# S5 inputs from x times g, the merge in two streams, and the recurrence's preparation cut into lanes of its own

## The chip, the cores and the metric

The kernel runs on one core of one Trainium2 chip. The metric is the device time of one execution in microseconds (us). TensorE (PE) does the matrix products; VectorE (DVE), ScalarE (ACT) and GpSimd (POOL) do the rest, and SyncE (SP) issues most of the transfers.

## The reference

One layer of a decoder, for 1024 tokens of width 1024 in float32:

```python
h = rms_norm(x, norm_mix_pre)              # x * rsqrt(mean(x*x) + 1e-6) * g, per token
proj = h @ w_in                            # columns: RWKV (1792), S5 input (512), gates (2048)
gates = sigmoid(proj[gate columns] + b_gate)
o_rwkv = rwkv7_branch(RWKV columns, ...) @ w_branch_rwkv
o_s5 = s5_branch(S5 columns, ...) @ w_branch_s5
mixed = (g_rwkv * o_rwkv + g_s5 * o_s5) @ w_out
x = x + rms_norm(mixed, norm_mix_post)
x = x + rms_norm(conv_ffn(rms_norm(x, norm_ffn_pre)), norm_ffn_post)
```

The RWKV-7 branch is a recurrence over the tokens with a 64x64 state for each of 8 heads. Each step scales the state by a decay, adds a product along a normalised key, and adds an outer product of value and key; then the state is multiplied by r. The S5 branch is a diagonal complex state space model (64 states for each group of 16 channels), followed by a GELU and a sigmoid GLU. The norm's factor 1/rms is one number per token, so h = (x * g) / rms, and a column of h @ w_in equals (x * g) @ w_in divided by rms afterwards.

## The kernel before

*Layout.* Activations lie channel-major: 128 channels on the partitions by 512 tokens, in two token halves (th = 0, 1). A product of float32 precision is made of three products of reduced width: each operand is split into a high part (a cast) and a low part (the difference), and PE adds hi*Whi, lo*Whi and hi*Wlo (`mm3_steps`, L171 to L173; the words "products" below are single ones of 128x128 by 128x512). Weights come through `load_w` (L143): a transfer, a cast on ACT (L155) and a subtraction on DVE (L156). Activations are split by `split` (L225, L226).

*Order.* PE executes in exactly the order in which the program emits its instructions. `drive` (L184) makes that order: it holds *lanes*, generators that each yield a PE cost and a latency (the constants T_... at the file's end, in us) or a condition. A lane whose latency has passed in the planner's own clock is continued; between lanes, the planner takes units of a background list, `fill`, one after the other, paced by PACE and CREDIT. If nothing is ready and fill is empty, the clock jumps. On the other engines a scheduler orders the instructions by dependence and priority (HP, HP2, HPW, HPN); each engine then executes its queue in order.

*Stages.*
1. Start (`load_x`, `norm`). x is loaded by SP, squared on ACT (L898), summed in pairs on DVE (L899) and over channels by PE (into the tile chk). From this the small steps of 1/rms are made, spread to a tile rbc, and DVE makes h = x * g * rbc (L908), which is split: high parts on ACT, low parts on DVE or, for every second tile, GpSimd.
2. S5 inputs (`s5_in`, L999): four column blocks of w_in times both halves of h, 192 products. ACT copies each result out with a change of layout (L1007); it is stored to DRAM, and SP reloads it as `u8` (`load_u8`) in S5's layout.
3. S5 itself (`s5_lane`, `tab_lane`): tables for each block (with transposes on PE at L543), then the state products. `mix_in` is the fill here: the projections of the RWKV columns, their low-rank second factors, and writing them to DRAM.
4. Recurrence. Four units i = 0..3, each for four heads (group i % 2) and one half (i // 2). For each there are: two *fronts* (`rwkv_front`, one per pair of heads u), which load r, k and v, normalise k and make the Gram products (L700) that DVE masks (L702); an *inverse* (`rwkv_inv`), which sends 32x32 blocks by transfers into another layout, runs 31 pairs of dependent DVE instructions (L757, L759), and sends the result back; the *natural layouts* (`rwkv_nat`), which are transposes on PE; the *level* step (`rwkv_level`), which begins with a DVE transpose of the inverse (L781) and joins 32-blocks to 64-blocks (L783 on PE); the *chain* (`rwkv_chain`) of eight dependent steps over 64 tokens each; and the *output* (`rwkv_out`) with a norm on DVE (L855) and transposes on PE (L861). `prep_lane` emits the fronts of unit i and, after the second, its inverse, and starts unit i+1's fronts only once the natural layouts of unit i are emitted. `chain_lane` emits natural layouts, level, chain and output in turn. The fill is the gate products (`gate_tiles`), and after the output of unit 1, `merge` and `outproj` for the first half.
5. `merge` (L1054) for the first half: eight tiles of the RWKV branch's projection times its gate, with the S5 GLU tiles put between, and then eight tiles of the S5 branch's projection times its gate, added to the first ones and split.
6. The second half's merge, the output projection, the norms and the gated FFN with its convolution. These stay as they are.

The two buffer pools `hp[0]` and `hp[1]` hold the split operands of each half, and the merge, the output projection and the fast FFN products use their slots again.

Of the kernel before, what the change touches and what calls it, by code (L numbers as in the profile page):

```python
# [9 lines left out]
F32 = mybir.dt.float32  # L10
# [60 lines left out]
class Kern:  # L71
# [71 lines left out]
    def load_w(self, *srcs):  # L143

        nc = self.nc
        wh, wl = [], []
        with self.tc.high_priority(HPW):
            for src in srcs:
                for o in range(0, src.shape[1], 512):
                    n = min(512, src.shape[1] - o)  # L150
                    h = self.wp.tile([128, 512], F32R, tag="wh", name=self.nm("wh"), bufs=NWH)
                    l = self.wp.tile([128, 512], F32R, tag="wl", name=self.nm("wl"), bufs=NWL)
                    f = self.wp.tile([128, 512], F32, tag="wf", name=self.nm("wf"), bufs=NWF)
                    nc.sync.dma_start(f[:, :n], src[:, o:o + n])
                    nc.scalar.copy(h[:, :n], f[:, :n])  # L155
                    nc.vector.tensor_tensor(l[:, :n], f[:, :n], h[:, :n].bitcast(F32), ALU.subtract)  # L156
                    wh.append(h)
                    wl.append(l)
        return wh, wl
# [114 lines left out]
    def setup(self):  # L274
        nc = self.nc
        self.vecs = self.const.tile([128, NVEC], F32, name="vecs")
        self.csts = self.const.tile([128, NCST], F32, name="csts")
        nc.gpsimd.dma_start(self.csts[:, 0:128], self.a["cst"][:, 0:128])
        nc.gpsimd.dma_start(self.vecs, self.a["vec"])
# [602 lines left out]
    def load_x(self, th, pool):  # L882
        xs = []
        for k in range(NK):
            x = pool.tile([128, 512], F32, name=self.nm("x"), tag="x", bufs=16)
            self.nc.sync.dma_start(x, self.a["x"][k * 128:k * 128 + 128, th * 512:th * 512 + 512])
            xs.append(x)
        return xs

    def norm(self, th, xs, pool):  # L890

        nc = self.nc
        ss = self.chk()[:, 0:512]
        yield 0, T_X
        for k in range(0, NK, 2):
            sq = [pool.tile([128, 512], F32, tag="sq", name=self.nm("sq"), bufs=4) for _ in range(2)]
            for i in range(2):
                nc.scalar.activation(sq[i], xs[k + i], AF.Square)  # L898
            nc.vector.tensor_tensor(sq[0], sq[0], sq[1], ALU.add)  # L899
            self.sumsq(ss, sq[0], k == 0)  # L900
            yield 0.9, 1.0
        bc = self.chk()[:, 0:512]
        self.spread(bc, self.rstd(ss, 1e-6, 1.0 / D))
        rbc = pool.tile([128, 512], F32, tag="rbc", name=self.nm("rbc"), bufs=1)
        nc.scalar.copy(rbc, bc)
        h = []
        for k in range(NK):
            nc.vector.scalar_tensor_tensor(xs[k], xs[k], self.vec("g_mix_pre", k), rbc, ALU.mult, ALU.mult)  # L908
            h.append(self.hsplit(xs[k], k, self.hp[th], eng=nc.gpsimd if k % 2 else nc.vector))
        self.h[th] = h  # L910
        yield 1.7, 5.0
# [45 lines left out]
    def rkv(self, p):  # L957

        for mt in (4 + p, p, 8 + p):
# [3 lines left out]
            yield from self.inproj((mt, use))  # L963

    def mix_in(self):
# [10 lines left out]
        self.load_u8(self.stored)  # L976
# [16 lines left out]

    def load_u8(self, b):

        self.nc.sync.dma_start(self.u8[b], self.US[b].rearrange("i c g n -> (i c) g n"))
        self.s5_in_done = b

    def s5_in(self, bs):  # L999

        w = [self.load_w(self.a["w_in"][14 + b]) for b in bs]
        for th in range(2):
            for b in bs:
                ps = self.gmp()
# [7 lines left out]
                if th:  # L1012
                    self.stored = b
# [750 lines left out]
NWH = 4  # L1764
# [80 lines left out]
```

## Time and profile before

| | |
|---|---|
| median of 3 runs | 1645.58 us (1643.46 to 1647.16) |
| profiled execution | 1646.42 us, of which 1644.6 us is the span |
| mean granted PE clock | 0.971 |
| PE busy | 1542.0 us, 94% of the span |
| PE weight loads (PEld) | 1240.8 us, 75% |
| DVE busy | 1132.4 us, 69% |
| ACT busy | 699.6 us, 43% |
| POOL busy | 134.6 us, 8% |
| transfers | 213.63 MB, mean 130 GB/s |

How to read it: "busy" is the time in which an engine has an instruction under way. L171 is line 171 of the kernel's file. In lists of instructions in order of time, a row has the start, the duration, the engine, the line, the operation, out<-in by the names of the tiles, the shapes, a count, and in brackets the idle time just before and what ended it (`<-ACT hh L225` is the ACT instruction that wrote hh). In lists of groups the columns are busy time and mean ns of one, and then the idle time of the engine before them and its main releaser. In lists of waits the columns are the total idle time, the number of waits and the longest. In stage lines the columns are the stretch, its length, busy time and instruction count of PE, PEld, DVE, ACT and POOL, the granted clock as a share of full speed, the busy share of the DMA engines, and GB/s. An engine's busy share over the whole span is an average over stages with different limits.

### The profile page before, as it was taken

Reading aid. Unit: us, or ns where it says so; the run is one execution under the profiler, and the core shown is the slowest. Engines: PE = TensorE matmul, PEld = TensorE weight load, DVE = VectorE, ACT = ScalarE, POOL = GpSimd, SP = SyncE. Lnnn points to the kernel's source line nnn. Section 1 sums busy time; section 2 is a strip of 40 time slices with the busy share of each in tenths; the row PEclk is TensorE's granted clock in tenths of the full one; section 3 lists DMA queues with packets and bytes.
Section 4 is the critical chain, followed back from the end, with each engine's and each line's share of the span. In section 5 each row is a group of like instructions: output and inputs, shape, how many; then the busy total and the mean of one; then the engine's idle time right before and its main releaser. Section 6 shows DMA issues by size and latency. Waiting matters only on the chain. (4 is left out here: it accounts for less than half of the span.)

```text
span 1644.6 us, 22694 instructions
## 1 busy us (share of the span) xinstructions
PE 1542.0 (94%) x8372; PEld 1240.8 (75%) x8372; DVE 1132.4 (69%) x2035; ACT 699.6 (43%) x1069; POOL 134.6 (8%) x190
## 2 busy tenths in 40 slices
PE   5899899899999998988999899999999999999995
PEld 4688787687777776666777688888888887788784
DVE  5898764555456456584379668977777777788667
ACT  4345543133243244344344445544454454443451
POOL 2100101312113123010000000000000000000000
PEclk9799999999999999998999999999999999999998
DMA  5254244333342354462167454322222224963632
GB/s 174 68 148 144 86 141 140 99 106 116 96 144 91 97 164 132 126 186 70 54 189 259 155 165 144 128 88 90 77 77 90 89 78 132 318 222 97 218 95 102
DMA packets 132382, 213.63 MB, mean 130 GB/s; under 512 B 38144, under 2 KB 44288, under 8 KB 132272
## 3 DMA queue, kind: packets, MB, share of 16 engines
q1 hardware_dynamic: 124208, 188.32, 36.6%
q0 software_dynamic: 6912, 21.77, 4.5%
q10 hardware_dynamic: 1152, 2.10, 0.3%
q8 instruction: 66, 1.08, 0.3%
q14 instruction: 44, 0.36, 0.1%
HBM read 156.56 MB, written 53.48 MB: 128 GB/s over the span
## 5 line engine op out<-in xcount | busy, mean ns | idle before, releaser
L171 PE MATMUL gm<-hh,wh 128*128 128x512 f32 x688 | 297.7, 433 | 8.6 <-ACT hh L225 4.2
L172 PE MATMUL gm<-hl,wh 128*128 128x512 f32 x688 | 276.2, 401 | 5.3 <-DVE hl L226 4.4
L173 PE MATMUL gm<-hh,wl 128*128 128x512 f32 x688 | 274.7, 399 | 0.0
L155 ACT CAST wh<-wf 128x512 fp32r<-128x512 f32 x179 | 111.0, 621 | 232.1 <-PE gm L172 147.3
L156 DVE TENSOR_TENSOR wl<-wf,wh 128x512 fp32r<-128x512 f32 x179 | 124.3, 695 | 113.5 <-ACT wh L155 109.4
L171 PEld LDWEIGHTS gm<-hh,wh 128*128 128x128 f32 x688 | 132.3, 192 | 45.1 <-ACT hh L225 6.2
L172 PEld LDWEIGHTS gm<-hl,wh 128*128 128x128 f32 x688 | 133.0, 193 | 32.0 <-DVE hl L226 7.3
L173 PEld LDWEIGHTS gm<-hh,wl 128*128 128x128 f32 x688 | 132.7, 193 | 29.3
L1470 PE MATMUL d<-xl,wh 128*128 128x512 f32 x308 | 121.0, 393 | 5.7 <-DVE xl L226 5.7
L1469 PE MATMUL d<-xh,wh 128*128 128x512 f32 x308 | 120.8, 392 | 2.1 <-ACT xh L225 2.1
L1471 PE MATMUL d<-xh,wl 128*128 128x512 f32 x308 | 120.5, 391 | 0.0
L1295 PE MATMUL rp<-t,h 128*128 128x512 f32 x216 | 84.4, 391 | 2.0 <-ACT p L1309 2.0
L1297 PE MATMUL rp<-t,l 128*128 128x512 f32 x216 | 84.2, 390 | 0.5 <-DVE l L226 0.5
L1296 PE MATMUL rp<-t,h 128*128 128x512 f32 x216 | 84.1, 389 | 0.0
L1470 PEld LDWEIGHTS d<-xl,wh 128*128 128x128 f32 x308 | 58.1, 189 | 19.4 <-DVE xl L226 7.4
L1469 PEld LDWEIGHTS d<-xh,wh 128*128 128x128 f32 x308 | 58.2, 189 | 14.6 <-ACT xh L225 2.4
L1471 PEld LDWEIGHTS d<-xh,wl 128*128 128x128 f32 x308 | 58.2, 189 | 12.0
L225 ACT CAST h<-r 128x1024 fp32r<-128x1024 f32 x34 | 35.9, 1055 | 61.1 <-PE rp L1296 29.6
L226 DVE TENSOR_TENSOR l<-r,h 128x1024 fp32r<-128x1024 f32 x34 | 41.7, 1225 | 29.3 <-ACT h L225 27.7
L1316 DVE SCALAR_TENSOR_TENSOR y<-zv,vecs,y 128x1023 f32<-128x1023 f32 (+1 forms) x36 | 46.1, 1280 | 8.6 <-ACT y L1314 8.6
L1295 PEld LDWEIGHTS rp<-t,h 128*128 128x128 f32 x216 | 40.5, 188 | 11.5 <-ACT p L1309 2.8
L1297 PEld LDWEIGHTS rp<-t,l 128*128 128x128 f32 x216 | 40.5, 188 | 9.4 <-DVE l L226 1.0
(435 smaller groups left out, 3358.9 us busy)
## 6 DMA issues: line engine op xcount, KB each, us to landing
r<-in_w_up_dram SPq DMA_DIRECT2D x36, 512.0 KB, 3.7
wf<-in_w_in_dram SPq DMA_DIRECT2D x68, 256.0 KB, 3.1
st<-in_w_down_dram SPq DMA_DIRECT2D x55, 256.0 KB, 4.3
st<-ACT SPq DMA_DIRECT2D x44, 256.0 KB, 4.7
wf<-in_w_up_dram SPq DMA_DIRECT2D x36, 256.0 KB, 2.8
ACT<-y POOLq DMA_DIRECT2D x18, 512.0 KB, 2.9
GT<-ev SPq DMA_DIRECT2D x32, 256.0 KB, 2.0
wf<-in_w_br_dram SPq DMA_DIRECT2D x32, 256.0 KB, 2.9
```

Of the source, the lines that this page charges most:

```text
L155: nc.scalar.copy(h[:, :n], f[:, :n])
L156: nc.vector.tensor_tensor(l[:, :n], f[:, :n], h[:, :n].bitcast(F32), ALU.subtract)
L171: mm(ps, a, xh[k], start=k == 0, stop=False)
L172: mm(ps, a, xl[k], start=False, stop=False)
L173: mm(ps, b, xh[k], start=False, stop=k == n - 1)
L1295: mm(ps, wh[:, c], xh, start=first and k == 0, stop=False, skip_group_check=True)
L1296: mm(ps, wh[:, c], xl, start=False, stop=False, skip_group_check=True)
L1297: mm(ps, wl[:, c], xh, start=False, stop=k == 3, skip_group_check=True)
L1316: V.scalar_tensor_tensor(y[:, lag:], z[:, 0:1024 - lag], self.vec(nme, i), y[:, lag:], ALU.mult, ALU.add)
L1469: mm(ps, wh[:, c], xh[:, x], start=start, stop=False, skip_group_check=True)
L1470: mm(ps, wh[:, c], xl[:, x], start=False, stop=False, skip_group_check=True)
L1471: mm(ps, wl[:, c], xh[:, x], start=False, stop=stop, skip_group_check=True)
```

## The change

*Start.* `start` takes the place of `load_x`, `norm`, `s5_in` and `load_u8`. The 192 S5 products no longer take h, but x * g, split into a high part made by ACT (an activation with scale g) and a low part made by DVE. DVE multiplies each result by rbc as it brings it out of PSUM (`store`), where ACT copied it before. The squares of all eight tiles are made on ACT and summed up one after the other on GpSimd, so that PE takes one sum over channels per half and not four. 1/rms of a half is made while the next half's products run, in two stretches of `norm`; h for the other projections is made as before, beside the later S5 products. The reload of `u8` is issued by GpSimd directly after the second half's store. The weights of a block come in two parts (`load_part`); the vectors are loaded ahead of the constants.

*Recurrence.* The inverse and the natural layouts get lanes of their own. A front of unit i+1 still waits for the natural layouts of unit i, but these are now emitted as soon as unit i's fronts are done and unit i-1's chain is emitted, so that the next front can be emitted while unit i's inverse runs. The first fronts also wait until the projections that they load are emitted (`rkv_done`). T_INV is 52 in place of 36.

*Merge.* `merge` becomes `merge_a` (S5 operands, GLU tiles, S5 projection times gate), a unit of fill behind the gate tiles, and `merge_b` (RWKV projection times gate, sum and split), which a lane puts into the fill 14 us of the planner's clock after the output of unit 1, with `outproj` behind it. The two pools change roles, so that the split operands of the merge lie in the other one.

```diff
-    def load_x(self, th, pool): ...
-    def norm(self, th, xs, pool): ...
-    def load_u8(self, b): ...
-    def s5_in(self, bs): ...
+    def start(self, pool):
...
+        def scaled(th, k):
+            hi, lo = self.pair(th, k)
+            g = self.vec("g_mix_pre", k)
+            A.activation(hi, xs[th][k], AF.Identity, scale=g)
+            V.scalar_tensor_tensor(lo, xs[th][k], g, hi.bitcast(F32), ALU.mult, ALU.subtract)
+            raw[th].append((hi, lo))
+        def square(th, k, acc):
+            sq = pool.tile([128, 512], F32, tag="sq", name=self.nm("sq"), bufs=4)
+            A.activation(sq, xs[th][k], AF.Square)
+            if acc is not None:
+                G.tensor_tensor(sq, sq, acc, ALU.add)
+            return sq
+        def normed(th, k):
+            x = xs[th][k]
+            V.scalar_tensor_tensor(x, x, self.vec("g_mix_pre", k), rbc[th], ALU.mult, ALU.mult)
+        def hsplit(th, k):
+            self.h[th][k] = self.hsplit(xs[th][k], k, self.hp[th], eng=G if k % 2 else V)
...
+        def store(b, th, ps):
+            y = self.ev((128, 8, 64))
+            V.tensor_tensor(y.rearrange("p i n -> p n i"), ps.rearrange("p (n j) -> p n j", j=8)[:, :, ::-1],
+                            rbc[th].rearrange("p (n j) -> p n j", j=8)[:, :, ::-1], ALU.mult)
+            sp.dma_start(self.US[b].rearrange("i c g n -> (c g) i n")[:, :, th * 64:th * 64 + 64], y)
+            if th:
+                G.dma_start(self.u8[b], self.US[b].rearrange("i c g n -> (i c) g n"))
+                self.s5_in_done = b
+        def norm(th, acc):
+            ps = self.chk()
+            self.sumsq(ps[:, 0:512], acc, True)
+            y = self.rstd(ps, 1e-6, 1.0 / D)
+            yield
+            self.spread(ps[:, 512:1024], y)
+            rbc[th] = pool.tile([128, 512], F32, tag="rbc", name=self.nm("rbc"), bufs=2)
+            A.copy(rbc[th], ps[:, 512:1024])
+            yield
...
+        acc = None
         for k in range(NK):
+            scaled(0, k)
+            acc = square(0, k, acc)
+        n0 = norm(0, acc)
+        p0 = self.gmp(), self.gmp()
+        for k in mms(w0, 0, p0):
+            pass
         for k in range(NK):
+            scaled(1, k)
+        p1 = self.gmp(), self.gmp()
+        for k in mms(w0, 1, p1):
+            if k in (1, 4):
+                next(n0)
+            if k == 3:
+                wload(w1, (16, 17), 0)
+        for b in range(2):
+            store(b, 0, p0[b])
+        acc = None
+        for k in range(NK):
+            acc = square(1, k, acc)
+            normed(0, k)
+        n1 = norm(1, acc)
+        wload(w1, (16, 17), 512)
+        p2 = self.chk()
+        p2 = p2[:, 0:512], p2[:, 512:1024]
+        for k in mms(w1, 0, p2):
+            hsplit(0, k)
+            if k in (1, 4):
+                next(n1)
+        for b in range(2):
+            store(b, 1, p1[b])
+        for b in range(2):
+            store(2 + b, 0, p2[b])
+        for k in range(NK):
+            normed(1, k)
+        p3 = self.gmp(), self.gmp()
+        for k in mms(w1, 1, p3):
+            hsplit(1, k)
+        for b in range(2):
+            store(2 + b, 1, p3[b])
...
-    def merge(self, mg): ...
+    def merge_a(self, first):
...
+        for m in range(4):
+            br.append(self.pair(0, 4 + m))
+            yield from self.glu_tile(m, xs, self.ev(), lambda: self.s5_y(self.ev(s8), m, 0), br[m])
+        for m in range(NK):
+            first.append(self.hp[1].tile([128, 512], F32, tag=f"h{'lh'[m // 4]}{m % 4}", name=self.nm("hl"), bufs=1))
+            yield from self.gate(1, m, 0, br, self.ev(), first[m])
+    def merge_b(self, first, mg):
...
         for m in range(NK):
             t = self.ev()
-            yield from self.gate(1, m, 0, br[4:8], t, t)
+            yield from self.gate(0, m, 0, br, t, t)
             nc.vector.tensor_tensor(t, t, first[m], ALU.add)
...
     def prep_lane(self, u):
         for i, d in enumerate(self.ds):
-            yield 0, lambda: self.nat >= i - 1
+            yield 0, lambda: self.nat >= i - 1 and self.rkv_done >= 2 * (i % 2) + u
...
             self.fronts += 1
-            if u:
-                yield 0, lambda: self.fronts == 2 * i + 2
-                with self.tc.high_priority(HPW):
-                    self.rwkv_inv(d)
-                yield 0, T_INV
-                self.prep = i
+    def inv_lane(self):
+        for i, d in enumerate(self.ds):
+            yield 0, lambda: self.fronts >= 2 * i + 2
+            with self.tc.high_priority(HPW):
+                self.rwkv_inv(d)
+            yield 0, T_INV
+            self.prep = i
+    def nat_lane(self):
+        for i, d in enumerate(self.ds):
+            yield 0, lambda: self.fronts >= 2 * i + 2 and self.chain >= i - 1
+            yield from self.rwkv_nat(d)
+            self.nat = i
+    def merge_lane(self, first, mg):
+        yield 0, lambda: self.outs >= 1 and self.merging
+        merge = self.merge_b(first, mg)
+        next(merge)
+        yield 0, T_MB
+        self.fill += [merge, self.outproj(0, mg, self.mx0)]
-    def chain_lane(self, mg):
+    def chain_lane(self):
         for i, d in enumerate(self.ds):
-            yield 0, lambda: self.prep >= i
-            yield from self.rwkv_nat(d)
-            self.nat = i
+            yield 0, lambda: self.prep >= i and (i < 3 or self.nat >= i)
...
             yield from self.rwkv_level(d)
+            yield 0, lambda: self.nat >= i
             yield from self.rwkv_chain(d)
+            self.chain = i
...
-            if i == 1:
-                self.fill += [self.merge(mg), self.outproj(0, mg, self.mx0)]
+            self.outs = i
-T_KN, T_BK, T_GR, T_INV, T_LV, T_CH, T_LN = 5.0, 9.0, 2.5, 36.0, 1.0, 0.8, 11.0
+T_MB = 14.0
+T_KN, T_BK, T_GR, T_INV, T_LV, T_CH, T_LN = 5.0, 9.0, 2.5, 52, 1.0, 0.8, 11.0
```

The emission order that results: of the new start, all 192 S5 products stand first, as before; 168 products of `mix_in` stand between them and the first S5 table, where 39 stood. In the recurrence, the second unit's fronts stand beside the first inverse, the third's in the second chain, and the fourth's beside the third level step and its chain's start. Behind the last output transposes the gate products of the second half's merge follow at once, where 30 other products stood between.

167 lines of the change are left out of this document (68 added, 99 removed).

## The prediction

> **What bounds the kernel now.** I read the page's first two parts, then the stages, then what TensorE (PE) waited for, then the order of time at the places found.
>
> ```profile
> span 1644.6 us, 22694 instructions
> PE 1542.0 (94%) x8372; PEld 1240.8 (75%) x8372; DVE 1132.4 (69%) x2035; ACT 699.6 (43%) x1069; POOL 134.6 (8%) x190
> DVE  5898764555456456584379668977777777788667
> PEclk9799999999999999998999999999999999999998
> ...
> 0.00:26.35 26.35, 9.20 (x40) 8.76 (x41) 9.37 (x30) 10.01 (x16) 2.31 (x12) 1.00 0.82 260
> 26.35:96.83 70.48, 61.36 (x232) 47.01 (x233) 62.70 (x202) 27.47 (x46) 12.54 (x10) 0.85 0.25 71
> 268.00:320.00 52.00, 43.83 (x226) 34.87 (x225) 28.00 (x63) 14.21 (x23) 18.07 (x24) 0.90 0.38 117
> ...
> 740.00:760.00 20.00, 15.77 (x118) 11.52 (x119) 11.41 (x18) 9.38 (x15) 0.00 (x0) 0.66 0.28 79
> ...
> 320.00:366.00 46.00, 46.00 (x219) 37.88 (x218) 24.72 (x80) 14.11 (x23) 7.63 (x13) 1.00 0.45 134
> 666.00:736.00 70.00, 61.43 (x392) 46.56 (x390) 51.75 (x139) 31.14 (x60) 9.05 (x13) 0.98 0.58 158
> 764.00:822.00 58.00, 58.00 (x460) 43.39 (x460) 18.28 (x40) 22.58 (x53) 0.00 (x0) 1.00 0.19 56
> ...
> PE chk L244 <- DVE sq L899: 12.6, 2, 11.1
> PE rp L700 <- DVE gr L702: 7.6, 2, 5.0
> PE mm L171 <- ACT t L230: 5.3, 2, 4.1
> PE chb L783 <- DVE ld L781: 5.1, 1, 5.1
> PE rp L861 <- DVE yn L855: 4.8, 1, 4.8
> ```
>
> The stage lines give the stretch and its length, the busy time of PE, PEld, DVE, ACT and POOL, then granted clock, DMA share and GB/s. PE is the bound, and its order is fixed, so a change gains only what PE loses: idle time, and products at half clock. The long losses stand at the start (26 us until the first projection product, then 70 us at a mean clock of 0.85), at the first recurrence input (268 to 320) and at the last one (666 to 736, with the waits of L783 and L861). Everything after the recurrence is unchanged in kind.
>
> The profiled execution took 1646.42 us (1644.6 span and 1.8 around it), 0.84 over the median of 1645.58; I sum against it and predict for the median.
>
> **The change, part by part.**
>
> *Start.* Before the change the norm must be known ahead of the first product.
>
> ```profile
> 7.87 0.63 ACT L898 ACTIVATE sq<-x 128x512 f32<-128x512 f32 x1 [2.56 <-DMA x<-in_x_dram]
> 26.35 0.80 PE L171 MATMUL gm<-hh,wh 128*128 128x512 f32 x1 [2.11 <-ACT hh L225]
> 96.83 0.39 PE L171 MATMUL gm<-hh,wh 128*128 128x512 f32 x1
> 105.22 0.39 PE L172 MATMUL gm<-hl,wh 128*128 128x512 f32 x1
> 105.45 0.40 PE L173 MATMUL gm<-hh,wl 128*128 128x512 f32 x1
> 105.68 1.04 PE L543 MATMUL chk<-csts,t 128*128 128x128 f32 x8
> ...
> L908 DVE SCALAR_TENSOR_TENSOR x<-x,vecs,rbc 128x512 f32<-128x512 f32 x16 | 15.4, 998 | 2.8 <-ACT rbc L905 2.8
> L899 DVE TENSOR_TENSOR sq<-sq,sq 128x512 f32<-128x512 f32 x8 | 5.5, 686 | 2.9 <-ACT sq L898 2.9
> L226 POOL TENSOR_TENSOR hl<-x,hh 128x512 fp32r<-128x512 f32 x8 | 11.6, 1461 | 53.9 <-ACT hh L225 53.9
> L1007 ACT COPY ev<-gm 128x512 f32<-128x512 f32 x8 | 8.7, 1092 | 13.2 <-PE gm L173 13.2
> ```
>
> Warm products start 0.227 us apart (105.22, 105.45). The 192 S5 products run from 26.35 to 96.83; at 105.68, after 39 products of the next stage, PE takes the first S5 table. After the change x lands as before (7.87), ACT scales it (0.63), DVE makes the low half (0.74 when undisturbed), so PE starts near 9 us. The first 48 products go at ACT's pace: 16 scalings and squares and 4 weight casts at some 0.6 are 12 us, so to 21.6. The next 48 take 10.9 and wait about 1 us for the first 1/rms; to 33.6. The third 48 carry the second 1/rms. DVE reaches that only behind 12 small steps, two evictions now on DVE (the ones of L1007) and eight L908: near 50, while PE comes to it at 41. PE loses 9 us, and half of the next 3 or 4; third group to 56, fourth to 67. Then the planner puts 168 products of the next stage (38 us) before the first S5 table: 105. DVE must by then have made the table. In the stretch from 26.35 to 96.83, which ended with that table, DVE worked 62.7. Of this four sums go (2.7); eight evictions come (7, an estimate just under ACT's 1.09 each), some nine evictions and weight splits of the next stage at 0.7 (6), and 7 for meetings with GpSimd (below): 80. DVE is through with the 16 scalings near 27, so the table stands at 107 (101 if nothing meets, 118 if every GpSimd sum does and pushes the second 1/rms). At that point 129 more products are done than before: 129 x 0.227 = 29.3, less 107 - 105.7: **minus 28** (minus 17 to minus 33). ACT loses the 8 evictions and gains 8 more casts' worth of scalings; it is idle in most of this stage (27.47 of 70.48 busy), so that is nothing.
>
> The sums of squares move from DVE (L899) to GpSimd, seven per half: 14 sums by 1.46 hidden behind the products, except for what they do to DVE:
>
> ```profile
> 24.90 2.08 DVE L908 SCALAR_TENSOR_TENSOR x<-x,vecs,rbc 128x512 f32<-128x512 f32 x3 [2.78 <-ACT rbc L905]
> 27.49 1.77 DVE L908 SCALAR_TENSOR_TENSOR x<-x,vecs,rbc 128x512 f32<-128x512 f32 x1
> 27.42 1.29 POOL L226 TENSOR_TENSOR hl<-x,hh 128x512 fp32r<-128x512 f32 x1 [24.04 <-ACT hh L225]
> ```
>
> Three L908 alone take 2.08, one that meets a GpSimd subtraction 1.77. That is 1.0 us for each meeting; I count 7 of the 14, since DVE waits for ACT during the first seven.
>
> The Trainium skill, GPSIMD Engine Reference, section 1, says that GpSimd shares its SBUF interfaces with VectorE, with contention for VectorE instructions that have two SBUF inputs; both operations here have two, and these rows agree. By that rule all 14 would cost DVE, 7 us more than I count: the table at 114 instead of 107, the sum 1630.
>
> The S5 input's reload now sits on the GpSimd queue, ahead of four subtractions (1.46 each) of the normalised second half; PE needs these only at about 72 us, and the reload waits for stores near 58. Nothing. Loading the vectors first, and renaming the two buffer pools, change no length.
>
> *First inverse.* Before, 168 pure products cover the wait. After, the layout transposes, 48 products and all of the second front stand there.
>
> ```profile
> 300.18 1.16 PE L700 MATMUL rp<-ar,bk 64*128 64x128 f32 x16
> 306.36 2.58 PE L700 MATMUL rp<-ar,bk 64*128 64x128 f32 x16 [5.01 <-DVE gr L702]
> 309.46 0.63 PE L172 MATMUL gm<-hl,wh 128*128 128x512 f32 x1
> 309.88 0.63 PE L173 MATMUL gm<-hh,wl 128*128 128x512 f32 x1
> ...
> 336.63 0.22 DVE L757 TENSOR_TENSOR tm<-x,mt 128x62 f32<-128x62 f32 x1
> 357.42 0.19 DVE L759 TENSOR_TENSOR x<-x,tm 128x16 f32<-128x16 f32 x1
> 366.08 0.70 DVE L781 STREAM_TRANSPOSE ld<-gr 32x512 f32<-32x512 f32 x1 [7.85 <-DMA gr<-xd]
> ```
>
> A front without a chain beside it, both halves at once, stalls 5.0 us at its Gram products, and the products after it stand 0.42 apart (309.46, 309.88), which is half clock; 0.90 over the 52 us is some 5 us below full, of which I count 3.4. The second front gets that too: **plus 8** (0, because inside the chain it also cost something, to 20, if DVE serves it late). It shares DVE with the inverse, whose 62 steps took 20.8 us undisturbed (336.63 to 357.42) and 46 with its transfers (320 to 366). A front's DVE work, about 19 us by rows like these, will stand between its steps one for one: 65 us. PE has 192 products (43.6), transposes (4.5), the front (6.7) and its stall (8): 63. So the level step waits **plus 2** (0 to 10). T_INV of 52 makes the planner leave room for part of it.
>
> *Last inverse.* Before, it took 70 us (666 to 736), because its steps meet the output norm and a merge on DVE (51.75 busy in 70). After, the last front ends 6.4 chain steps before the third chain's end, not 4.6: with 58 us for 8 steps (764 to 822) that is 13 us earlier. Of what stands there (4.8 at L861, 5.1 at L783, and 6 at half clock, as 740 to 760 at 0.66 shows) I take **minus 8** (minus 16 to plus 10: the merge's S5 half now lies beside that front, and its sums still meet the output norm).
>
> *End.* 30 products that stood behind the last output transposes now stand ahead: the gate products follow at once and find their operands late, as at L171 (4.1): **plus 3** (0 to 8).
>
> *Sum.* 1646.4 - 28 + 8 + 2 - 8 + 3 = 1623.4, so 1623 for the median.
>
> **The rivals.**
> 1. *The start's gain is partly swallowed by GpSimd.* If all sums collide, and the second 1/rms comes later with them, the table stands at 118 and the gain is 17: 1634. For it, the 1.77 row; against it, DVE's waits for ACT early on. The Trainium skill's rule above (GPSIMD Engine Reference, section 1) leads this way.
> 2. *DVE becomes the bound beside the last front.* Four S5 output splits and four GLU tiles, each with a weight split, join the front there; if that costs 10 instead of giving 8, the time is 1641. For it 51.75 of 70 busy; against it 18.28 of 58 in the chain that follows.
> 3. *The other side: the first inverse runs late.* Front and inverse alternate on an engine that serves in order; when a Gram result is late, the inverse behind it is late, and all chains with it. It costs what the last inverse shows, 70 us, plus a whole front, 19, against 63 of cover: 26, with half clock 30, in place of my 2; with the front's stall at 20 and the last inverse gaining nothing, 1646 - 28 + 20 + 30 + 3 = 1671, and with the last inverse as I have it 1663. It turns the sign when the two waits together pass 33 us. For it: PE stands still for 5 us with DVE only half busy (28.00 of 52). Against it: the first inverse has neither the output norm nor a merge beside it, which the last had.
> 4. *It does not do what it says:* the table is DVE's, not PE's, and comes so late (130) that the 129 products bring 5 us, which the other terms take back: 1646.
> 5. *Everything falls well:* no meeting, no second stall, no late operands at the end: 1646 - 33 - 14 = 1599.
>
> **How the numbers follow.** My forecast (1612 to 1632) 0.46, rival 1 (1632 to 1640) 0.13, rival 2 (1636 to 1643) 0.08, rival 3 0.18, rival 4 0.06, rival 5 0.09. Within 0.2% (3.3 us, about what this kernel's spread of 1643.46 to 1647.16 can tell) holds rival 4. Faster 0.75, same 0.06, slower 0.19. The likeliest alone is 1612 to 1632; leaving out the lower half of rival 5 and most of rival 3, I get 1604 to 1654.
>
> **What the profile would show.** First projection product by 10 us, the first S5 table transpose at 101 to 118 with 168 products of the next stage ahead of it; a wait of TensorE for the small rms steps in the third group; about 16 scalings of DVE, several at 1.77. A second Gram wait of some 5 us with half clock in the first inverse; the level step's wait for the DVE transpose in the first recurrence under 10 us, and that in the last gone. It is wrong if the first table comes after 125, if a wait over 15 us stands at the first level step, or if DVE is over 90% busy around the last front with PE idle.

## The result and the profile after

The changed kernel takes 1671.56 us (median of four runs, 1665.8 to 1674.98); beside it the kernel before took 1646.34. The ratio is 1.0153, with a 95% interval of 1.0134 to 1.0172: slower by 1.5%, where 1623 was forecast. The profiled execution took 1674.98 us, of which 1673.2 is the span.

The first two parts of the page of the changed kernel:

```profile
span 1673.2 us, 22652 instructions
PE 1549.2 (93%) x8324; PEld 1242.8 (74%) x8324; DVE 1154.2 (69%) x2051; ACT 696.6 (42%) x1073; POOL 161.9 (10%) x208
DVE  7998874562544474584368668977777776778767
PEclk9999999899989995997999899999999999899998
```

The busy shares hardly move; the clock row does, with slices of 5 and 7 at about 630 and 750 us; the mean granted clock is 0.951, and was 0.971. The stage lines of the changed kernel (columns as before):

```profile
9.30:33.00 23.70, 22.33 (x86) 16.93 (x86) 22.73 (x18) 19.80 (x35) 17.69 (x12) 1.00 0.60 203
38.60:115.70 77.10, 72.56 (x306) 59.06 (x307) 75.46 (x226) 32.79 (x57) 16.85 (x14) 0.93 0.43 134
307.30:396.80 89.50, 76.18 (x409) 60.21 (x408) 50.97 (x133) 21.24 (x36) 32.23 (x43) 0.89 0.42 121
622.80:665.60 42.80, 35.93 (x202) 24.58 (x202) 19.52 (x25) 17.78 (x26) 7.71 (x6) 0.53 0.38 101
755.40:788.90 33.50, 30.30 (x203) 22.43 (x204) 15.36 (x21) 16.00 (x23) 2.59 (x4) 0.74 0.39 91
1421.40:1430.60 9.20, 0.18 (x1) 0.00 (x0) 7.95 (x8) 3.90 (x5) 0.00 (x0) 0.67 0.88 283
```

The first products and the first S5 table come as the chain of steps had it, though the table later:

```profile
9.30 0.80 PE L931 MATMUL gm<-hh,wh 128*128 128x512 f32 x1 [9.30 <-ACT hh L905]
115.74 1.03 PE L546 MATMUL chk<-csts,t 128*128 128x128 f32 x8
```

Three of the stages are new costs. The first inverse (307.3 to 396.8) takes 89.5 us at clock 0.89. The third level step up to its chain (622.8 to 665.6) takes 42.8 us at clock 0.53. At 1421.4, in a stage that was not to change, PE stands still for 9.2 us. The stage lines of the kernel before for the first two of these:

```profile
300.20:370.50 70.30, 65.28 (x331) 52.62 (x330) 37.23 (x100) 16.70 (x27) 13.82 (x21) 0.95 0.38 109
603.20:623.10 19.90, 19.90 (x194) 14.81 (x193) 5.75 (x16) 7.56 (x13) 3.96 (x6) 1.00 0.56 181
```

The groups of waits of the changed kernel name them (us in total, times, longest):

```profile
PE chb L786 <- DVE ld L784: 13.1, 3, 5.8
PE gm L931 <- ACT hh L905: 9.3, 1, 9.3
PE d L1537 <- ACT wh L228: 9.0, 1, 9.0
PE rp L864 <- DVE yn L858: 8.2, 1, 8.2
PE rp L703 <- DVE gr L705: 7.4, 2, 6.5
PE gm L174 <- ACT hh L1103: 6.3, 2, 4.0
PE rp L703 <- DVE bk L691: 5.3, 1, 5.3
```

To add all stages up I use one measure, *lost time*. For each pair of successive PE instructions it is the distance between their starts, less the usual distance for that line and shape (the lower quartile in the same trace). What a stretch lost is its length less the sum of those usual distances; each stretch begins where the one above it ends, and the last one ends with PE's last instruction. It holds idle time, half clock, and small products that wait on each other.

| stretch (us lost) | before | changed | new start alone | fronts after inverse | three mended | three mended, sums on DVE |
|---|---|---|---|---|---|---|
| to the first S5 table | 44.5 | 30.5 | 32.2 | 29.9 | 28.2 | 26.7 |
| to the first Gram products | 17.4 | 10.9 | 8.3 | 10.6 | 10.6 | 8.5 |
| to the first level step | 15.3 | 34.7 | 15.3 | 15.1 | 15.3 | 15.0 |
| to the second level step | 26.7 | 25.0 | 25.5 | 25.9 | 26.1 | 26.1 |
| to the second output | 25.3 | 31.4 | 29.7 | 30.4 | 30.1 | 30.3 |
| to the third level step | 2.4 | 5.6 | 19.2 | 13.2 | 13.2 | 13.1 |
| to the third chain | 2.9 | 25.9 | 2.8 | 2.7 | 2.7 | 2.8 |
| to the fourth chain | 53.2 | 46.3 | 48.8 | 38.5 | 38.3 | 38.7 |
| to the fourth output | 15.0 | 15.0 | 21.2 | 30.7 | 33.8 | 30.7 |
| to the fast FFN products | 24.6 | 26.7 | 28.3 | 30.0 | 29.0 | 28.6 |
| to the down-projection | 6.3 | 13.7 | 6.0 | 12.0 | 6.7 | 6.8 |
| to the end | 13.8 | 15.0 | 14.0 | 13.6 | 14.3 | 11.5 |
| sum | 247.4 | 280.7 | 251.3 | 252.6 | 248.3 | 238.8 |

Between before and changed the loss grows by 33.3 us; the sums over channels that PE no longer makes take 5 off its work, and the span grows by 28.6.

### The profile page after: what moved, and what is told of

The parts are those of the page before. It is cut to its first block, busy times and chain, and to the rows that moved or that the text cites. A ratio compares the mean times of both kernels' runs of the same rounds, so it can differ in the third digit from the quotient of the medians.

```text
span 1673.2 us, 22652 instructions
## 1 busy us (share of the span) xinstructions
PE 1549.2 (93%) x8324; PEld 1242.8 (74%) x8324; DVE 1154.2 (69%) x2051; ACT 696.6 (42%) x1073; POOL 161.9 (10%) x208
## 5 line engine op out<-in xcount | busy, mean ns | idle before, releaser
L174 PE MATMUL gm<-hh,wh 128*128 128x512 f32 x624 | 275.2, 441 | 9.7 <-ACT hh L1103 6.3
L175 PE MATMUL gm<-hl,wh 128*128 128x512 f32 x624 | 252.9, 405 | 0.8 <-DVE hl L1104 0.6
L176 PE MATMUL gm<-hh,wl 128*128 128x512 f32 x624 | 252.5, 405 | 0.0
L160 DVE TENSOR_TENSOR wl<-wf,wh 128x512 fp32r<-128x512 f32 x179 | 128.2, 719 | 140.4 <-ACT wh L159 129.5
L174 PEld LDWEIGHTS gm<-hh,wh 128*128 128x128 f32 x624 | 121.3, 194 | 43.2 <-ACT hh L1103 7.7
L176 PEld LDWEIGHTS gm<-hh,wl 128*128 128x128 f32 x624 | 122.1, 196 | 27.7
L175 PEld LDWEIGHTS gm<-hl,wh 128*128 128x128 f32 x624 | 122.4, 196 | 22.9 <-issue 1.9
```

The costliest lines, as they stand in the source:

```text
L174: mm(ps, a, xh[k], start=k == 0, stop=False)
L175: mm(ps, a, xl[k], start=False, stop=False)
L176: mm(ps, b, xh[k], start=False, stop=k == n - 1)
```

## The experiments

Three theories stand in the expectations. Theory A: the start's gain reaches the end, and the changed kernel is slower by separate costs behind it (first inverse, S5 operands, pools). Theory B: these add up, stage by stage. Theory C, the rival that grew out of the first runs: the recurrence takes the start's gain back, because the ready products that cover its waits run out earlier. In the runs on the start alone and on the background, "theory B" is only the name of the rival that is written beside it.

**The pools.** Edit, on the changed kernel:

```diff
-                    self.hp = (hp0, hp1)
+                    self.hp = (hp1, hp0)
```

> The changed kernel with the two buffer pools in each other's place in memory, so that the pool that the fast FFN products hold to their end is again the one that lay where it lay before the change. Theory A (the exchange of the pools makes the first down-projection weights wait for the end of the fast products): their transfers stand ahead of the ACT reloads again, the 9.2 us wait of TensorE ahead of the first down product falls to 2 to 3, and the time is 1671.6 - 7 = 1664.5. Rival (the wait is an accident of transfers in one run): the wait varies, and the time stays at 1671.

Measured: 1663.21, ratio to before 1.0110 (1.0074 to 1.0147). This interval overlaps that of the changed kernel, so the reading rests on the trace. The transfers that SyncE issued at that place, with start and time; before the change, changed, and with this edit:

```profile
1380.48 3.18 SPq L1394 DMA_DIRECT2D A<-in_w_down_dram  x7
1387.95 3.39 SPq L1400 DMA_DIRECT2D st<-ACT  x7
```

```profile
1408.86 3.17 SPq L1468 DMA_DIRECT2D st<-ACT  x7
1418.89 2.69 SPq L1468 DMA_DIRECT2D T<-ACT  x6
1423.55 3.44 SPq L1462 DMA_DIRECT2D A<-in_w_down_dram  x7
1430.62 0.79 PE L1537 MATMUL d<-xh,wh 128*128 128x512 f32 x1 [9.04 <-ACT wh L228]
```

```profile
1397.79 3.17 SPq L1462 DMA_DIRECT2D A<-in_w_down_dram  x7
1405.25 3.48 SPq L1468 DMA_DIRECT2D st<-ACT  x7
```

In the changed kernel the weights A are issued behind both reloads of ACT, at 1423.55, and PE waits 9 us for them. With the pools exchanged back they are first again, the 9 us wait is gone, and the stretch loses 7.9 instead of 13.7. Of the table's runs with the next edit, it loses 12.0 without the exchange and 6.7 with it. The reason is read from the kernel's text, since no trace shows addresses: the first pool of the down-projection is laid where `hp0` lay, and the changed `fast_weights` and `keep` hold `hp[0]` to their end. A change of names moved a lifetime onto other memory.

**The fronts beside the inverse.** Edit, on the changed kernel, in `prep_lane`:

```diff
-            yield 0, lambda: self.nat >= i - 1 and self.rkv_done >= 2 * (i % 2) + u
+            yield 0, lambda: self.nat >= i - 1 and self.prep >= i - 1 and self.rkv_done >= 2 * (i % 2) + u
```

> The changed kernel with one condition more: a unit's fronts begin only when the planner takes the inverse of the unit before as done, so the second fronts no longer stand beside the first inverse. Theory A (the front's DVE work between the inverse's steps makes the first level step late): first inverse 21 us on DVE instead of 34, the stretch from the first Gram product to the first level step 89.5 falls to about 70 to 75, of which 5 come back as front work in the first chain: 1671.6 - 12 = 1660. Rival (the allowance of 52 us for the inverse puts the level step there, not DVE): stretch still near 89, 1671.

Measured: 1645.97, ratio 1.0008 (0.9988 to 1.0028). By the ratios that is 24 us off the changed kernel, twice what was expected of it. The stretch to the first level step:

```profile
306.40:384.80 78.40, 73.39 (x367) 59.34 (x366) 35.50 (x90) 20.27 (x33) 14.68 (x23) 0.96 0.41 125
```

It is 11 us shorter with more full-size products in it (268 for 221), and its loss is 15.1, as before the change. The rest comes at the third level step (2.7 lost for 25.9), because the fourth fronts no longer stand there together with the S5 operands. Of the 43 us that these two places give, some 16 are lost again ahead of the fourth output (30.7 for 15.0).

But the first level step of the changed kernel did not wait at all. What was late was the second front itself: PE waited 5.3 us for its operand bk (L691, in the list of waits above), and each Gram wait halved the clock again. In the changed kernel DVE came to bk like this:

```profile
370.19 1.85 DVE L712 SCALAR_TENSOR_TENSOR ld<-ld,vecs,ld 128x512 f32<-128x512 f32 x1 [2.37 <-POOL ld L693]
372.16 0.68 DVE L691 SCALAR_TENSOR_TENSOR bk<-gr,ld 128x512 f32<-128x512 f32 x1
```

DVE itself stood idle for 2.4 us until a product on GpSimd was done, for an instruction (L712) that the Gram products do not need and that stood ahead of bk in its queue. The inverse's steps lie between the front's instructions too. The run removes all of this together, so it shows what the front costs at this place, and not how the cost divides.

**The S5 operands.** Edit, on the changed kernel: the lines of `merge_a` that make `xs` become `s5_operands`, called by the last gate tile behind its first half.

```diff
             self.nc.sync.dma_start(self.GT[m][:, th * 512:th * 512 + 512], t)
+            if m == 15 and th == 0:
+                self.s5_operands()
...
-        xs, br = [], []
-        for b in range(4): ...
+        xs, br = self.s5x, []
```

> The changed kernel with the S5 operands of the merge made between the two halves of the last gate tiles, 48 products ahead of their use, instead of right ahead of it. Theory A (TensorE waits for these operands during the third level step, twice, and each wait keeps the clock at half for some 15 us more): the stretch from the third level step to the third chain falls from 42.8 us to 25 to 28, and the time is 1671.6 - 15 = 1656. Rival (the clock is at half there because of the level step's own wait before it): only the two waits go, 7 us: 1664.

Measured: 1659.71, ratio 1.0082 (1.0050 to 1.0114): 12 us better, between the two. In the changed kernel PE asks for these operands right behind the last gate product, and waits for ScalarE's cast of them (the second time ScalarE had itself waited 2.9 us for the transfer that brings them):

```profile
641.70 0.80 PE L174 MATMUL gm<-hh,wh 128*128 128x512 f32 x1 [4.02 <-ACT hh L1103]
646.29 0.79 PE L174 MATMUL gm<-hh,wh 128*128 128x512 f32 x1 [2.28 <-ACT hh L1103]
```

With the edit both waits go, and the stage falls from 42.8 to 30.5 us at clock 0.69. Theory A and its rival are both right in part. In the changed kernel the clock is at half from 622.4 to 663.2, so it fell at the level step's own wait (4.2 us, until 622.8), and the two later waits made the half clock longer. With the edit it is at half from 619.1 to 639.4. The stage does not reach 25, because the splits of S5 now stand ahead of the level step's transposes on DVE, so that the wait before that step grew to 9.5:

```profile
623.90:654.40 30.50, 28.98 (x204) 21.23 (x204) 15.54 (x20) 10.31 (x19) 6.45 (x5) 0.69 0.41 116
618.22 4.99 DVE L1106 TENSOR_TENSOR hl<-ld,hh 128x512 fp32r<-128x512 f32 x3 [0.48 <-ACT hh L1105]
623.13 1.28 DVE L784 STREAM_TRANSPOSE ld<-gr 32x512 f32<-32x512 f32 x2
623.88 1.05 PE L786 MATMUL chb<-ld,gr 32*32 32x32 f32 x16 [9.51 <-DVE ld L784]
```

**The start alone.** The kernel before with `start`, `load_part`, the order of the vectors and nothing else of the change.

> The kernel before with the new start alone; recurrence and merge as they were. Theory A (the start gains what the trace shows up to the first Gram product, some 25 us of TensorE work, and what makes the changed kernel slower lies behind it): 1646 - 25 = 1621, with the first S5 table near 116 behind 168 products. Rival (the recurrence is bound by its own serial chain; work done earlier only empties the background that covers its waits, so that the gain is lost there): first S5 table near 116 as well, but 1640 to 1646, with new waits at the level steps.

Measured: 1644.67, ratio 0.9994 (0.9976 to 1.0011). No gain at all, with a first S5 table at 117.3 and 21 us less lost up to the first Gram products. The end time is the rival's, though the waits do not stand at the level steps, as it had them: of those 21 us, 17 are lost again between the second output and the third level step (19.2 for 2.4), and the rest ahead of the second output and around the fourth. Between the second output and the third level step the stage line and two rows of PE are:

```profile
596.20:629.00 32.80, 22.03 (x81) 15.37 (x81) 17.97 (x28) 22.45 (x33) 7.92 (x13) 0.80 0.79 210
602.91 0.80 PE L174 MATMUL gm<-hh,wh 128*128 128x512 f32 x1 [2.75 <-ACT hh L228]
619.48 0.89 PE L734 MATMUL rp<-csts,bk 128*128 128x128 f32 x4 [4.67 <-ACT bkn L735]
```

The gate products, whose operands have been ready since the start, are now used up at the second output. The merge has to follow at once, and its operands are what that output has just written: they go through DRAM, ScalarE and DVE, and ScalarE is then late for the natural layouts too. To test this, work that waits for nothing was added:

```diff
-... [self.gate_tiles(m) for m in range(14)] + ...
+... [self.gate_tiles(m) for m in (*range(2), *range(14))] + ...
```

> The kernel before with the new start (1644.7), and with the first two gate tiles computed and stored twice: 96 products more, 21.8 us of TensorE work that waits for nothing, put into the background ahead of the others. Theory C (the start's gain is lost because the gate products, which need nothing from the recurrence, now run out before the second output has made the merge's operands): the extra work fills just those waits and costs next to nothing, 1644 to 1650, and the stretch from the second output to the third level step loses under 5 us to waits and half clock, not 19. Theory B (the gain is lost elsewhere, TensorE being the bound): 1666.

> Control for the run beside it: the kernel before with the same 96 products more. Theory C: before the change the gate products last just long enough, so that more of them only adds work: 1644.5 + 21.8 = 1666, a few us less if they cover waits of the fourth front. Theory B: 1666 as well. If it is far under that, the kernel before is not bound by TensorE there either, and theory C says too little.

Measured: 1650.32 with the new start, ratio 1.0018 (0.9999 to 1.0037), and 1658.61 without it, ratio 1.0058 (1.0038 to 1.0078). 21.8 us of extra PE work cost the new start 4 us (0.24% from 0.9994), and the stage is as it was before the change:

```profile
594.20:609.10 14.90, 14.46 (x82) 11.45 (x80) 5.70 (x14) 8.01 (x13) 5.15 (x8) 1.00 0.58 169
```

So the 17 us at this place were lost for want of ready work. That is not yet the start's whole gain. With the extra work 86 us are lost from the third level step to the fourth output, for 73 with the new start alone: part of the loss moves one unit on. And the control missed: before the change the same work costs some 10 us and not 22, so that kernel has waits that ready work covers, too. One such stretch is from the third to the fourth chain (47.4 lost for 53.1); but its profiled execution also lost 5 us less in the start, which the edit does not touch, so the rest is not settled. With the extra work in both kernels the new start is worth some 7 us (ratio 1.0018 for 1.0058), and not the 26 that it saves up to the first Gram products (21 less lost and 5 less work). Where the remainder goes was not tested further.

**A smaller share of background.** With the new start, without it, and with the three edits above together:

```diff
-PACE, CREDIT = 0.8, 2.0
+PACE, CREDIT = 0.6, 2.0
```

> The kernel before with the new start, and with the planner's background per unit of recurrence work cut from 0.8 to 0.6: per unit of the recurrence some 40 products (9 us) fewer stand between fronts, level step and chain, so that the background lasts longer. Theory C (the start's 21 us are lost because the same background per unit is used and runs out one unit early): the 25 us of waits and half clock around the second output fall, recurrence units get shorter, 1625 to 1632. Theory B (the start's gain is lost to something else, DVE or the merge's operands): 1644 as with 0.8.

> The kernel before, with the background per unit of recurrence work cut from 0.8 to 0.6, as a control. Theory C: without the new start the background is enough at 0.8, so what is left over is only done later: 1640 to 1648. If the smaller share is a gain in itself, whatever the start does: below 1635, and the gain of the run beside it isn't the start's.

> The three edits together, with the share of background at 0.6. Theory C: the gain of the start and of the mended waits appear together: 1615 to 1625. Theory B: the share makes no difference, as with the three edits alone: 1630.

Measured: 1657.50 (ratio 1.0086, 1.0071 to 1.0101), 1647.57 (1.0032, 1.0016 to 1.0047) and 1663.68 (1.0126, 1.0106 to 1.0145). Only the control came out as expected; the theory failed as a recipe. With the new start the loss around the second output did go (2.4), but the background now changed from gate tiles to merge one stage later, beside the fourth front, and these waits of PE came:

```profile
PE rp L864 <- DVE yn L858: 12.6, 1, 12.6
PE gm L174 <- ACT hh L228: 9.3, 2, 8.1
PE rp L703 <- DVE bk L691: 8.2, 1, 8.2
```

By these waits it counts not only how much ready work is left, but also what DVE has to do at the place where it ends; no run changed the second alone.

**The sums on DVE.** With the new start alone, in `square`:

```diff
-                G.tensor_tensor(sq, sq, acc, ALU.add)
+                V.tensor_tensor(sq, sq, acc, ALU.add)
```

> The kernel before with the new start, whose sums of squares are made by DVE and not by GpSimd: 14 sums of 0.69, 9.7 us more for DVE, and no GpSimd instruction beside the 16 scalings, which took 19.6 us in the changed kernel (1.23 each) against 0.74 each undisturbed, 7.8 us less. If what GpSimd costs DVE is as large as that, the first S5 table stands within 2 us of 117; if most of the stretching has another cause, it comes 8 to 10 us later, at 125. The end time stays near 1645 either way, as work ahead of the recurrence is lost again there.

Measured: 1641.12, ratio 0.9949 (0.9932 to 0.9966), with the table at 113.6, even earlier than 117. The table's place is as expected if GpSimd costs DVE that much; the end time is not, since 1645 was expected and the gain of 0.45% is clear of the noise. The groups of the first 60 us, of the changed kernel and with this edit:

```profile
L906 DVE SCALAR_TENSOR_TENSOR hl<-x,vecs,hh 128x512 fp32r<-128x512 f32 x16 | 19.8, 1294 | 1.5 <-ACT hh L905 1.5
L913 POOL TENSOR_TENSOR sq<-sq,sq 128x512 f32<-128x512 f32 x14 | 21.7, 1550 | 12.1 <-ACT sq L911 11.3
```

```profile
L906 DVE SCALAR_TENSOR_TENSOR hl<-x,vecs,hh 128x512 fp32r<-128x512 f32 x16 | 11.3, 746 | 0.9 <-ACT hh L905 0.9
L913 DVE TENSOR_TENSOR sq<-sq,sq 128x512 f32<-128x512 f32 x14 | 9.6, 684 | 0.0
```

DVE's scalings lose 8.5 us by meeting GpSimd; doing the sums itself costs DVE 9.6. GpSimd took over nothing, and needed 1.55 for what DVE does in 0.68. That this gain was not lost again, as the start's was, fits what differs between the two. PE's order is the same instruction for instruction in both runs, so no ready product is used earlier; the new start, in contrast, puts 144 more products ahead of the first Gram products than the kernel before (942 for 798).

**Together.** The three edits (pools, fronts, S5 operands) on the changed kernel; the same with only the second unit's fronts held; the three with the sums on DVE; and this last with `T_INV` at 36. The second and the fourth:

```diff
-... self.nat >= i - 1 and self.prep >= i - 1 and ...
+... self.nat >= i - 1 and (i != 1 or self.prep >= 0) and ...
-T_KN, T_BK, T_GR, T_INV, T_LV, T_CH, T_LN = 5.0, 9.0, 2.5, 52, 1.0, 0.8, 11.0
+T_KN, T_BK, T_GR, T_INV, T_LV, T_CH, T_LN = 5.0, 9.0, 2.5, 36.0, 1.0, 0.8, 11.0
```

> The changed kernel with all three edits together: pools exchanged back, S5 operands made between the halves of the last gate tiles, second fronts held until the inverse before them is done. Theory B (the three costs stand in different stages and add): 1646 of the last edit alone, less 6 to 7 for the down-projection weights, less 7 to 10 for the waits for S5 operands and the half clock behind them: 1630. Theory C (the recurrence's serial chain and its background set the end): the down-projection's 6 to 7 are kept, since they lie behind the recurrence, but the S5 operands' gain only lengthens a later wait: 1639.

> The changed kernel with the pools exchanged back, the S5 operands early, and only the second unit's fronts held until the first inverse is done; the third and fourth unit's fronts begin as in the changed kernel. If the first inverse is the only place where a front beside an inverse costs: as the three edits together or a little faster, 1630 to 1638. If every front beside an inverse or a level step costs: slower than the three edits together, 1640 to 1650.

> The three edits together (1638), with the sums of squares on DVE. Alone with the new start that move gave 0.45%, 4 of it up to the first Gram product. If it is independent of the merge and the recurrence: 1631 to 1634. If the recurrence takes it back, as it took the start's gain: 1638.

> The same, with the planner's allowance for an inverse back at 36 from 52: 72 products fewer stand beside the first inverse and 45 fewer beside each later one, and the background reaches through the fourth chain, where the three edits together lose 13 us to waits in each of the two stretches around the fourth output. Theory C (what counts is that the background lasts until the last chain's end): those 13 us go, the level steps wait some 2 to 5 each instead, 1622 to 1630. If a shorter cover beside the inverses costs as much at the level steps, or if the merge meets the fourth front as with the smaller share: 1635 to 1645.

Measured: 1638.23 (ratio 0.9966, 0.9950 to 0.9982), 1652.71 (1.0028, 1.0008 to 1.0048), **1634.40** (0.9923, 0.9898 to 0.9948) and 1668.86 (1.0138, 1.0114 to 1.0162). The first is theory C's number, and the third is close to what was expected if the move to DVE is independent of the rest. The second and the fourth lie above all that was expected of them. The third is faster than both kernels, by 0.8% against before. The edits do not add: by the ratios they gave 7, 24 and 12 us alone and 31 together, since with the fronts held the S5 operands no longer stand at the bad place. With the three edits the background is used up in the fourth chain:

```profile
779.10:844.20 65.10, 56.20 (x409) 45.80 (x408) 27.11 (x61) 22.51 (x52) 0.00 (x0) 0.71 0.27 77
```

Holding only the second unit's fronts is not enough: with the fourth fronts free again, 18.1 us are lost from the third level step to its chain, in place of 2.7. And with the allowance at 36 the fourth chain is covered again (15.0 lost), but with 72 and then 45 products fewer beside each inverse PE waits at the level steps, and it is the worst of the four:

```profile
PE chb L786 <- DVE ld L784: 33.2, 5, 8.6
```

## Why the prediction was wrong

The sum had minus 23, and the profiled execution of the changed kernel took 28.6 more: 51.6 apart. The step that failed most is "last inverse and last front": the third level step, with the fourth fronts and the S5 operands beside it, has no term of its own, and it took 23.0. The second front beside the first inverse was 11.4 too small, the pools at nothing were 7.4, and the waits from the first level step to the third were 5.6 too small. The other steps differ by 4 in all. By its own steps, in the lost time of the table:

- *Start, minus 28.* Measured 20.5 less lost up to the first Gram products and 5 less work of PE: minus 25, inside its range. The table stood at 115.7, 8.7 later than forecast: DVE was at work for 86.6 us between 27 and the table, where the sum had 80. Rival 1's mechanism is real: DVE was slowed where it met GpSimd. I had 7 us for it and none of it for the first seven sums; the scalings alone lost 8.5. The Trainium skill (GPSIMD Engine Reference, section 1) says that GpSimd contends with VectorE instructions that have two SBUF inputs; the groups agree, 1294 against 746 ns.
- *Second front beside the first inverse, plus 8.* Measured 19.4 in that stretch. The mechanism was the one named, a second stall and half clock: the first front stalled for 6.5 us and the second for 5.3, each with half clock behind it (0.89 over 89.5 us, and 0.95 over 70.3 when the first fronts stood alone). Mis-sized, at the upper bound of 20. The second stall was for bk, and not for DVE's mask as the first.
- *First level step waits, plus 2.* It did not: the inverse's steps took 34.5 us (346.8 to 381.3) with the front between them, and not the forecast 20.8 plus 19. The second level step waited 5.8, which was not in the sum. The stretches from the first level step to the third lost 62.0 for 54.4 before, plus 7.6.
- *Last inverse and last front, minus 8.* From third to fourth chain the loss fell by 6.9, near the forecast, but in part by luck. The two waits that it was to be taken from were 8.2 (L864) and 3.2 (L786), 11.4 together, for 9.9 before, and the last level step's wait, which was to be gone, was not. But the price was paid one stage earlier: from the third level step to its chain, plus 23.0. Rival 2 had named the S5 splits and the front beside each other, and gave them 18 us in all. This is the largest error: I priced that place by DVE's share of a stretch, and not by the first operand that PE would ask for with nothing left to cover it.
- *End, plus 3.* Measured 2.1.
- *Pools, "change no length".* Measured plus 7.4. This was costed at nothing without a look at what is laid on that memory next.

Rival 3 gave the right time, 1663 to 1671, and the sign by the right pair (front and inverse on one DVE). That the time fits is luck: its 30 us for the first level step did not come, and about as much came at the third level step and the down-projection, of which it says nothing. None of the three signs by which the prediction would be wrong appeared either: the table came at 115.7, the first level step did not wait, and DVE was busy for 20.4 of the 35 us around the last front (655 to 690).

The error that the terms do not show is the model: *PE is the bound, so a change gains what PE loses*. The new start alone has lost 21 us less at the first Gram products and is equal at the end. PE was fully busy in the middle of the recurrence because ready products stood there, and the start took its gain out of that same stock. The run with the extra work shows this for 17 of the 21 us at one place; that all of the gain is lost this way is argued from the sums on DVE, and not shown.

## What to carry to other kernels

Where a planner covers the latencies of a serial stage with ready work, that work is a stock. Time that is gained by doing some of it earlier has to be followed to the point where the stock runs out; time that was gained here without touching the order was kept. Where it runs out, price the first operand that TensorE will ask for, not an engine's mean share. Before renaming or exchanging buffers, look at what the next pools are laid on.

## What the runs showed of the hardware

A wait of PE costs more than its length, and how much depends on what follows it. Stage lines for two waits, the second level step with `T_INV` at 36 and the down-projection of the changed kernel:

```profile
482.80:486.00 3.20, 0.07 (x1) 0.00 (x0) 0.94 (x2) 0.00 (x0) 1.66 (x3) 0.94 0.90 266
486.00:490.60 4.60, 0.00 (x0) 0.00 (x0) 1.83 (x3) 0.62 (x1) 2.58 (x4) 0.50 0.62 168
490.60:516.00 25.40, 25.38 (x151) 18.78 (x152) 3.90 (x15) 4.95 (x8) 1.18 (x1) 0.50 0.24 79
516.00:522.00 6.00, 6.00 (x53) 4.57 (x52) 1.24 (x2) 0.58 (x1) 1.18 (x1) 0.97 0.21 69
```

```profile
1421.40:1425.00 3.60, 0.18 (x1) 0.00 (x0) 3.60 (x5) 2.15 (x4) 0.00 (x0) 0.92 0.88 279
1425.00:1430.60 5.60, 0.00 (x0) 0.00 (x0) 4.34 (x4) 1.74 (x2) 0.00 (x0) 0.50 0.88 285
1430.60:1434.60 4.00, 3.94 (x8) 2.65 (x9) 3.86 (x4) 2.52 (x3) 0.00 (x0) 0.50 1.05 399
1434.60:1440.00 5.40, 5.40 (x25) 4.48 (x24) 5.40 (x7) 1.73 (x2) 0.53 (x1) 0.99 1.04 394
```

In both the granted clock halves some 3 us into the wait (0.94 over 3.2 us and 0.92 over 3.6 are 2.8 and 3.0 us at full clock). It is not always as long: in the changed kernel PE stood still from 490.57, ahead of the second level step, and the clock was at half from 492.6, after 2.0 us. With full-size products behind the wait (the down-projection), it is back after 4.0 us of work. Behind the level wait, where 32x32 products stand between the full ones, it stays at half for 25.4 us although PE is busy throughout: a wait of 7.7 us cost some 10 more (12.4 lost from there to the second chain, against 2.9 with the allowance at 52). The Trainium skill (TensorE: Matmul & The Clock Gate, Part 1: The HAM clock gate) gives about 3.4 us of idle for the drop and about 3.4 us of sustained work for the return. The drops here come earlier than that; the return behind the down-projection's wait is near it (4.0), and the one behind the level step's wait is not (25.4). That the small products keep the clock down is an inference from where they stand; no run changed them alone.
